# Transposing an 8192 x 8192 matrix: the loads move from ScalarE's DMA queue to SyncE's

## The chip, the core and the metric

The kernel runs on one core of one Trainium2 chip. The metric is device time in microseconds (us) of one execution, as the median of several runs. The core has a matrix engine (TensorE, PE in the profile), a vector engine (VectorE, DVE), a scalar engine (ScalarE, ACT), GpSimd (POOL) and a synchronising engine (SyncE, SP). Each works through its own list of instructions in order, and semaphores hold them together. Data moves between the main memory and the core's SBUF through 16 DMA engines. A transfer is issued by an instruction of SyncE or ScalarE and goes into that engine's queue: q1 in the profile is SyncE's, q10 is ScalarE's.

## The reference

```python
x = np.random.randn(8192, 8192).astype(np.float32)

def reference(x):
    return np.transpose(x)
```

The matrix has 268.44 MB. Each byte is read once and written once, so 536.87 MB pass through the DMA engines.

## The kernel before, in words

**Tiling.** `x` is cut into chunks of 128 rows by 4096 columns (2 MB). There are 64 chunks down (index `c`) and 2 sweeps across (index `s`), so T = 128 chunks, taken in order, a sweep at a time. A chunk is loaded with one DMA into one of three input buffers `in0` to `in2` (`load`, L100 to L104): each of the 128 partitions gets one row piece of 16 KB.

**TensorE.** `transposes` (L111 to L123) waits until the chunk's buffer is loaded (`s_ld`, L112), then makes 32 transposes of 128 x 128 through the identity matrix. They go in 8 groups of 4. Groups 0 to 3 fill the PSUM tile `ps0`, groups 4 to 7 `ps1`. Before each half it waits until the tile has been emptied (`s_bank`, L116). After each second group it counts up `s_pe`, so `s_pe` grows by 4 a chunk.

**Copies and bands.** A group is a band: 512 columns of `x`, so 512 rows of `out`. A band is gathered over 8 consecutive chunks in one of nine SBUF registers (`regs`, 2 MB each), so that a row piece of `out` in it is 4 KB long and the four rows of a partition make a run of 16 KB in SBUF. ScalarE copies bands 0 to 3 from `ps0`, VectorE bands 4 to 7 from `ps1` (L228). The bands are staggered: at each chunk one of the eight closes. In the first chunks of all and in the last ones they close with fewer chunks, hence the smaller stores of the profile, and at the change of sweep a register can hold parts of two sweeps, which are stored by two DMAs. A band that begins again takes the register that has been free longest, and its first copy waits until the store out of that register has landed (`s_st`, L202). Eight bands are open and there are nine registers, so this is the store issued two chunks before.

**Stores.** `store` (L160) is called in the order of the code right after the copies that close a band. ScalarE waits for the copy, its own or VectorE's (`s_cp`, L162), and issues the DMA into q10. The helper `wide_dma` (L28) writes the instruction directly, so that the source is one run of 16 KB in each partition; the first store of all uses the plain call (L174).

**The order around the change.** The program is unrolled in Python over the 128 chunks. For each chunk, ScalarE's list holds: its copies, the stores that close, then the wait for TensorE to have finished the chunk (L242), and the load of chunk t + 3 into the buffer that has just been read (L102). The first three loads are issued by SyncE at the start; all other loads, and all stores, are issued by ScalarE into one queue. At the end SyncE waits for the last stores (L245).

```python
            if t + NIN < T:
                nc.scalar.wait_ge(s_pe, (t + 1) * NR // 2)
                load(t + NIN)
```

The functions in full:

Of the kernel before, what the change touches and what calls it, by code (L numbers as in the profile page):

```python
# [40 lines left out]
def kernel(  # L41
# [13 lines left out]
    nc = tc.nc  # L55
# [8 lines left out]
    NR = S // B  # L64
    NIN = 3
# [4 lines left out]
    with tc.tile_critical():  # L70
# [12 lines left out]
        s_pe = nc.alloc_semaphore("s_pe")  # L83
# [15 lines left out]

        def load(t):  # L100
            s, c = chunks[t]
            (nc.sync if t < NIN else nc.scalar).dma_start(  # L102
                out=ins[t % NIN], in_=x[c * P:(c + 1) * P, s * J:(s + 1) * J]
            ).then_inc(s_ld[t % NIN], 16)  # L104

# [46 lines left out]
        for t in range(NIN):  # L152
            load(t)
# [6 lines left out]
        def store(q, e, count):  # L160
            t0, r, parts = window.pop(q)
            nc.scalar.wait_ge(s_cp[e], count)  # L162
            base = 0
            for s, a, z in parts:
                rows = (z - a) * P
                j0 = s * J + q * B * P
                dst = out[j0:j0 + B * P, a * P:a * P + rows]
                dst = dst.rearrange("(q b) i -> q b i", q=P)
                src = regs[:, r * SIZE + base:r * SIZE + base + B * rows]
                base += B * rows  # L170
                if any(stored):
                    st = wide_dma(nc, nc.scalar, "qActDynamicHW", dst, src)
                else:
                    st = nc.scalar.dma_start(  # L174
                        out=dst, in_=src.rearrange("q (b i) -> q b i", b=B)
                    )
                st.then_inc(s_st[r], 16)
                stored[r] += 1
            free.append(r)

        def closes(w, t):
            t0, r, parts = w
            return t + 1 == t0 + sum(z - a for _, a, z in parts)

        for t, (s, c) in enumerate(chunks):
            for e in range(2):
                eng = (nc.scalar, nc.vector)[e]

                place = []
                for q in range(e * NH, (e + 1) * NH):  # L190
                    if q not in window:

                        span = (q - c) % W + 1
                        r = free.pop(0)
                        parts = [(s, c, min(c + span, CH))]
                        if c + span > CH and t + span < T:
                            parts.append((s + 1, 0, c + span - CH))
                        window[q] = (t, r, parts)  # L200
                        if stored[r]:
                            eng.wait_ge(s_st[r], 16 * stored[r])  # L202
                    t0, r, parts = window[q]
                    k = [p[0] for p in parts].index(s)
                    base = r * SIZE + B * P * sum(z - a for _, a, z in parts[:k])
                    _, a, z = parts[k]
                    place.append((base + (c - a) * P, (z - a) * P))

                runs = []
                for g in range(NH):  # L210
                    if runs:
                        u = runs[-1]
                        gap = place[g][0] - place[g - 1][0]
                        if place[g][1] == place[u[0]][1] and abs(gap) < 2 ** 15 and (
                            len(u) == 1 or gap == place[u[1]][0] - place[u[0]][0]
                        ):
                            u.append(g)
                            continue
                    runs.append([g])
                for u in runs:  # L220
                    off, dist = place[u[0]]
                    gap = place[u[-1]][0] - place[u[-2]][0] if len(u) > 1 else 0
                    dims = [list(regs.ap[0]), [gap, len(u)], [dist, B], [1, P]]
                    o = bass.AP(regs.tensor, regs.offset + off, dims)
                    i = pss[e][:, u[0] * B * P:(u[-1] + 1) * B * P]
                    i = i.rearrange("p (l b i) -> p l b i", b=B, i=P)
                    eng.wait_ge(s_pe, t * NH + (e * NH + u[-1]) // 2 + 1)  # L227
                    cp = nc.scalar.copy(out=o, in_=i) if e == 0 else nc.vector.tensor_copy(out=o, in_=i)  # L228
                    ends = [e * NH + g for g in u if closes(window[e * NH + g], t)]
                    if ends:  # L230
                        cp.then_inc(s_cp[e], 1)
                        copied[e] += 1
                    if u is runs[-1]:
                        if ends:
                            eng.wait_ge(s_cp[e], copied[e])
                            eng.sem_inc(s_bank[e], 1)
                        else:
                            cp.then_inc(s_bank[e], 1)
                    for q in ends:
                        store(q, e, copied[e])  # L240
            if t + NIN < T:
                nc.scalar.wait_ge(s_pe, (t + 1) * NR // 2)  # L242
                load(t + NIN)
        for r in range(NREG):
            nc.sync.wait_ge(s_st[r], 16 * stored[r])  # L245
# [30 lines left out]
```

## Time and profile before

| what | value |
|---|---|
| median of 3 runs | 1263.75 us (1263.48 to 1265.18) |
| profiled execution, first to last instruction (span) | 1261.2 us |
| moved by DMA | 536.97 MB, mean 426 GB/s |
| read from, written to main memory | 268.44 MB, 268.44 MB |
| busy: PE, DVE, ACT | 59%, 24%, 20% |
| loads by ScalarE | 125 of 2 MB, 21.7 us from issue to landing (median) |
| loads by SyncE | 3 of 2 MB, 11.6 us |
| full stores | 114 of 2 MB, 17.5 us |
| smaller stores | 28, of 256 KB to 1792 KB |

The span is shorter than the time of a run, which also holds what lies before the first and after the last instruction; the page gives no other time of the profiled execution. The page has the span in 40 equal slices: a digit is the busy share of an engine in tenths, the row DMA the mean busy share of the 16 DMA engines, the row GB/s what they moved. The queue table lists packets, MB and the share of 16 engines' time that the packets took. A packet is one row of a transfer, here 16 KB in the steady part; a record of 4 bytes ends each engine's part of a DMA and counts up its semaphore. In the table of waits a row names the engine and line that waited, what it waited for, the total in us, how often, and the longest.

### The profile page before, as it was taken

The numbers are of one execution on the slowest core, as the hardware profiler recorded it, in microseconds if no ns is written. First come the engines' busy times: TensorE is split into PE (matmuls) and PEld (weight loads), VectorE is DVE, ScalarE is ACT, GpSimd is POOL, SyncE is SP. The second block draws the span as 40 slices with busy tenths as digits, with TensorE's granted clock in tenths as the row PEclk, the third lists the DMA queues.
The fourth block names the chain that finished last, engine by engine and source line by source line (L and its number), as shares of the span: only waits on it lengthen the run. The fifth ranks groups of instructions, "written<-read, shape, count | busy, mean of one in ns | idle before, by whom it ended". The sixth has DMA issues, their size and how long they took to land. (4 is left out here: it accounts for less than half of the span.)

```text
span 1261.2 us, 9840 instructions
## 1 busy us (share of the span) xinstructions
PE 740.3 (59%) x4096; PEld 719.8 (57%) x4096; DVE 302.7 (24%) x250; ACT 252.6 (20%) x257; POOL 0.7 (0%) x6
## 2 busy tenths in 40 slices
PE   6555655665556565665555655656566655656561
PEld 6555555665556555655555655656566655656561
DVE  3322222222222222222222222222222222222220
ACT  3212121121111211122211121121111211122120
POOL 0000000000000000000000000000000000000000
PEclk9987867777776868687776777676867677777866
DMA  9999999999999999999999999999999999999998
GB/s 386 429 427 426 430 427 429 431 428 430 431 428 431 429 429 430 430 429 430 425 423 419 431 430 429 430 430 429 431 430 429 431 429 430 430 430 429 429 429 351
DMA packets 39273, 536.97 MB, mean 426 GB/s; under 512 B 4320, under 2 KB 4832, under 8 KB 6240
## 3 DMA queue, kind: packets, MB, share of 16 engines
q10 hardware_dynamic: 38832, 530.60, 98.9%
q1 hardware_dynamic: 432, 6.29, 1.2%
q14 instruction: 8, 0.07, 0.0%
q8 instruction: 1, 0.02, 0.0%
HBM read 268.44 MB, written 268.44 MB: 426 GB/s over the span
## 5 line engine op out<-in xcount | busy, mean ns | idle before, releaser
L118 PE MATMUL ps<-ident,in 128*128 128x128 f32 x4096 | 740.3, 363 | 492.9 <-PEq L116 492.9
L118 PEld LDWEIGHTS ps<-ident,in 128*128 128x128 f32 x4096 | 719.8, 220 | 513.2 <-issue 513.2
L228 DVE COPY regs<-ps 128x512 f32<-128x512 f32 (+3 forms) x250 | 302.7, 1246 | 932.4 <-PE ps L118 780.2
L228 ACT COPY regs<-ps 128x512 f32<-128x512 f32 (+3 forms) x256 | 251.3, 1015 | 980.9 <-PE ps L118 495.5
L228 ACT ACT_TABLE_LOAD x1 | 1.3, 1283 | 0.9 <-SPq L70 0.9
L88 POOL TENSOR_SCALAR_AFFINE_SELECT ident<-ident 128x128 f32<-128x128 f32 x1 | 0.3, 292 | 0.2 <-POOL ident L86 0.2
L86 POOL MEMSET ident<- 128x128 f32 x1 | 0.2, 204 | 0.5 <-SPq L70 0.5
L260 POOL MEMSET const-bfloat16-1.0<- 128x1 bf16 x1 | 0.1, 101 | 0.0
L260 POOL MEMSET const-uint8-127<- 128x1 uint8 x1 | 0.1, 101 | 0.0
L260 POOL MEMSET const-float32-0.0<- 128x1 f32 x1 | 0.1, 98 | 0.2 <-issue 0.2
L260 POOL MEMSET const-float32-1.0<- 128x1 f32 x1 | 0.1, 98 | 0.0
## 6 DMA issues: line engine op xcount, KB each, us to landing
in<-in_x_dram ACTq DMA_DIRECT2D x125, 2048.0 KB, 21.7
out_dram<-regs ACTq DMA_DIRECT2D x114, 2048.0 KB, 17.5
out_dram<-regs ACTq DMA_DIRECT2D x4, 1792.0 KB, 17.1
in<-in_x_dram SPq DMA_DIRECT2D x3, 2048.0 KB, 11.6
out_dram<-regs ACTq DMA_DIRECT2D x4, 1536.0 KB, 15.2
out_dram<-regs ACTq DMA_DIRECT2D x4, 1280.0 KB, 15.5
out_dram<-regs ACTq DMA_DIRECT2D x4, 1024.0 KB, 15.6
out_dram<-regs ACTq DMA_DIRECT2D x4, 768.0 KB, 16.5
```

What stands on the lines that cost most here:

```text
L86: nc.gpsimd.memset(ident, 0.0).then_inc(s_id, 1)
L88: nc.gpsimd.affine_select(out=ident, in_=ident, compare_op=mybir.AluOpType.not_equal, fill=1.0, base=0, pattern=[[-1, P]], channel_multipl ...
L118: tr = nc.tensor.transpose(pss[e][:, (g * B + b) * P:(g * B + b + 1) * P], ins[k][:, q * B * P + b:(q + 1) * B * P - B + b + 1:B], ident,)
L228: cp = nc.scalar.copy(out=o, in_=i) if e == 0 else nc.vector.tensor_copy(out=o, in_=i)
L260: nc = _bacc.Bacc("TRN2", target_bir_lowering=False, num_devices=1)
```

## The change

All loads are issued by SyncE, into its own queue. The wait for TensorE, which tells that the input buffer has been read, moves to SyncE with them. Stores stay with ScalarE.

```diff
         def load(t):
             s, c = chunks[t]
-            (nc.sync if t < NIN else nc.scalar).dma_start(
+            nc.sync.dma_start(
                 out=ins[t % NIN], in_=x[c * P:(c + 1) * P, s * J:(s + 1) * J]
             ).then_inc(s_ld[t % NIN], 16)
...
             if t + NIN < T:
-                nc.scalar.wait_ge(s_pe, (t + 1) * NR // 2)
+                nc.sync.wait_ge(s_pe, (t + 1) * NR // 2)
                 load(t + NIN)
```

ScalarE's list loses 125 load instructions and the waits before them. SyncE's list grows from 3 loads to 128, with 125 waits between them. The lists of TensorE, VectorE and GpSimd are the same as before. Each of the 16 DMA engines then has packets of two queues, q1 (loads) and q10 (stores), where it had those of q10 alone once the first three loads were through.

## The prediction

> **What bounds the kernel now.** I read the page's slices and queue table first, because the busy shares of the engines (PE 59%, DVE 24%, ACT 20%) leave no engine as the bound.
>
> ```profile
> DMA  9999999999999999999999999999999999999998
> GB/s 386 429 427 426 430 427 429 431 428 430 431 428 431 429 429 430 430 429 430 425 423 419 431 430 429 430 430 429 431 430 429 431 429 430 430 430 429 429 429 351
> ...
> q10 hardware_dynamic: 38832, 530.60, 98.9%
> q1 hardware_dynamic: 432, 6.29, 1.2%
> ```
>
> The sixteen DMA engines are busy in every slice, at 429 to 431 GB/s outside a few slices, and nearly all of it is one queue, q10, that of ScalarE. q1 is SyncE's: the first three loads.
>
> Next the waits. They say whether a chunk (2 MB in, 2 MB out) waits for anything that is not a transfer.
>
> ```profile
> DVE regs L228 <- PE ps L118: 780.2, 120, 13.2
> PEld ps L118 <- issue: 513.2, 127, 8.4
> ACT regs L228 <- PE ps L118: 495.5, 100, 9.2
> PE ps L118 <- PEq L116: 492.9, 127, 8.5
> ACT regs L228 <- DMA out_dram<-regs: 473.9, 60, 10.4
> DVE regs L228 <- DMA out_dram<-regs: 152.1, 23, 7.8
> ```
>
> TensorE waits 127 times, once a chunk, for the next load; the copies wait for TensorE or for an old store. All of it ends in a transfer. The timeline shows one chunk:
>
> ```profile
> 600.53 6.49 PE L118 MATMUL ps<-ident,in 128*128 128x128 f32 x32 [3.50 <-PEq L116]
> ...
> 606.00 2.48 DVE L228 COPY regs<-ps 128x512 f32<-128x512 f32 x4 [7.32 <-PE ps L118]
> 608.52 0.55 ACTq L28 DMA_DIRECT2D out_dram<-regs  x1
> 609.11 0.62 ACTq L102 DMA_DIRECT2D in<-in_x_dram  x1
> 610.27 5.21 PE L118 MATMUL ps<-ident,in 128*128 128x128 f32 x32 [3.26 <-PEq L116]
> ```
>
> The period is 610.27 - 600.53 = 9.74 us, and 4.194 MB in 9.74 us is 430.6 GB/s: the chunk is the transfer. 128 chunks of 9.74 are 1246.7 of the span of 1261.2.
>
> Last the packets. In the trace's packet records one engine's share of a chunk is 8 load and 8 store packets of 16 KB, back to back. A load packet takes 611 ns; a store packet takes 611 ns for the first two of a DMA and 616 for the other six. So **the time of one 16 KB packet is the kernel's time**: 1 ns on each of the 16 costs 128 x 16 = 2.05 us.
>
> **The change, part by part.** Arithmetic, sizes, packets and buffers stay; the instruction order of TensorE, VectorE and GpSimd stays too.
>
> *Issues.* 125 loads leave ScalarE's order (637 ns median, 4589 longest, L102) and go to SyncE, where the first three took 372 to 426 ns each. One issue in 9.74 us hides there. Behind SyncE's new wait (the count s_pe, L242) stand only later loads and the last waits for stores, which nothing else needs. ScalarE gets back under 1 us in most chunks, but its copies already wait 473.9 us for stores and 495.5 for TensorE: worth 0. If that cover were gone, it would be 0.6 us a chunk.
>
> *Load earlier.* L102 stands behind a store that needs VectorE's copy, so at 609.11 it comes 2.1 us after TensorE is through (600.53 + 6.49 = 607.02). SyncE issues it at about 607. It then lies behind other packets anyway (21.7 us from issue to landing, of which its own 2 MB take 4.9): worth 0. Only the start has a hole that this might fill: 21 to 24 us runs at 328 GB/s, which is (430 - 328)/430 x 3 = 0.7 us. The packets there are slow (839 ns in 22 to 23 us), not missing, so I take 0 and keep 0.7 for the range.
>
> *Stores.* Nine registers serve eight open bands, so the copy of chunk t needs the store of chunk t - 2. A store may take about two periods less the copies, 19.5 - 3 = 16.5 us, and takes 17.5 now. With two queues its 8 packets alternate with loads, 16 x 0.61 = 9.8 us plus what stores are ahead: it lands sooner. An engine idles only if both its queues are empty. Loads have three buffers, of which TensorE holds one for 6 us in 9.74, so their queue stays full. Worth 0.
>
> *Alternation.* This term decides, and the steady trace has no example. The nearest rows are two.
>
> First, at 15 to 17.8 us the last of SyncE's loads meet the first store, ScalarE's 512-byte packets, on the same engines.
>
> ```profile
> 3.00:14.00 11.00, 5.54 (x33) 5.57 (x34) 0.78 (x2) 2.15 (x4) 0.00 (x0) 1.00 1.00 429
> 14.00:18.00 4.00, 4.00 (x34) 3.83 (x32) 2.61 (x5) 2.15 (x4) 0.00 (x0) 1.00 0.96 378
> ```
>
> (Columns: window, its length, busy us of five engines, clock, DMA share, GB/s.) The packet records show one packet of one queue, then one of the other. 72 load packets end in this stretch, mean 633.3 ns; the 296 before it had 611.7. So **21.6 ns a load packet**. The store packets cost what all 512-byte packets cost, 27 ns. Most of the extra sits at one place: 13 packets that start at 15.3 to 15.65 us carry 1461 of the 1604 ns by which the 72 are over 611, the other 59 next to nothing.
>
> Second, eight instruction fetches of 8 KB (q14) fall among q10's packets after the start. Each took 309 ns, and the q10 packet that came next took 796 to 1039 ns: 185 to 428 above 611, mean 301. This is the dear end: a return to a queue after a large packet of another.
>
> The ends: nothing (the others of the 72), and 301 ns at each return, which would be 301 x 2 x 8 x 128 = 617 us. The first row excludes the latter, since there alternating returns cost almost nothing. I take its mean, for it is the nearest: two hardware queues, a load and a store. 125 loads x 8 packets x 21.6 ns = **+21.6 us**. I give stores nothing extra; the same price for them would add another 21.
>
> The Trainium skill, "DMA: Bandwidth & Descriptors", section "Queues, rings and completion order", puts the switch elsewhere: the engine leaves a queue only at packet boundaries, and a packet is typically 9 to 17 descriptors. By that a DMA's share of eight rows would go through whole, there would be an eighth of the switches, and this term would be 21.6 / 8 = 2.7 us, an estimate from that page. The records speak against it: in the stretch with both queues each 16 KB row was followed by a row of the other queue, so the sum keeps 21.6.
>
> *What alternation gives back.* The slower store packets come only after two stores in a row; with a load between them they should all take 611. 10,121 packets had 616: x 5 ns / 16 engines = **-3.2 us**.
>
> *Sum.* +21.6 - 3.2 = +18.4 on the span of 1261.2: 1279.6. The median of the runs, 1263.75, lies 2.55 above the span; the profile's page has no other time of this execution, so I take these 2.55 as what lies around it. **1282 us**, 1.5% slower.
>
> **Rivals.**
>
> *Alternation is free: faster.* The price of 21.6 was one event at the first store, not one at every switch. Without it the extra is (1604 - 1461)/(72 - 13) = 2.4 ns a load packet, 2.4 us in all, against -3.2 and up to -0.7 for the start: 1262.2; with none at all 1263.75 - 3.9 = 1259.9. For it: the plain 611s in the alternating stretch. Against it: those store packets were 512 bytes and left the load stream almost whole. It decides when the extra of a load packet is under 1.4 ns, since 1000 of them in a row on an engine make 1.0 us a ns and 3.9 - 1.4 is the 2.5 us that can be told. Chance 0.15.
>
> *No change.* All issues end on the same engines, packets have the same bytes, and 611 and 616 stay as they are: within 2.5 us of 1263.75. The Trainium skill, "DMA: Bandwidth & Descriptors", section "Issuing engines are not separate DMA queues", has this as its rule: transfers from several issuers interleave on the same engines and only issue time is saved. The trace agrees on the same engines and on the interleaving, not on the rate, which is 378 against 429 in the one window with both queues. Chance 0.2.
>
> *Reads and writes in mixture cost more: clearly slower.* Today the engines mostly load together, then store together. Where they drift apart there are clusters of packets of 700 to 1700 ns:
>
> ```profile
> 200.00:600.00 400.00, 239.34 (x1312) 232.73 (x1312) 97.05 (x77) 79.23 (x73) 0.00 (x0) 0.75 1.01 430
> 640.00:690.00 50.00, 28.68 (x159) 27.84 (x158) 12.23 (x17) 9.39 (x6) 0.00 (x0) 0.71 1.01 419
> ```
>
> At 419 throughout: 1246.7 x (430/419 - 1) = +32.7, so 1296. If one queue ran dry once a chunk and its return cost 301 ns, it would be 128 x 0.301 = +38.5, so 1302. Both: 1335. Against: between 700 and 1200 us one engine is 5.3 us behind the rest (the spread of a DMA's sixteen completions), loads beside their stores, and the rate is 430 still. Chance 0.2.
>
> *The change doesn't take hold*, because SyncE issues late or both share a queue: q1 exists and carried its loads at 429 GB/s. Chance under 0.01, within "no change".
>
> **Chances and range.** The forecast (some price per switch, 1267 to 1290) 0.45, with the rivals at 0.2 clearly slower, 0.2 the same, 0.15 faster. A difference under 0.2% (2.5 us) is about what a measurement of this kernel cannot tell from no change. So slower 0.65, same 0.2, faster 0.15. The range reaches down to 1259, the free case with all gains, and up to 1322, between one of the dear costs and both.
>
> **What would show it.** Queue table: q1 and q10 at about half the packets each. Landing: stores fall from 17.5 us, loads stay near 21. If the forecast is right, DMA stays at 9 in every slice while GB/s falls to about 423, and 16 KB packets average some 10 ns more in the steady part. If a queue runs dry, the DMA share drops. If alternation is free, store packets are 611 and the chunk period is 9.71 us. The forecast is wrong if 16 KB stores beside loads cost either nothing or much more than 512-byte ones, which no row of this trace shows.

## The result and the profile after

The changed kernel took 1274.8 us in the median of 13 runs (1265.31 to 1276.88), the kernel before 1264.4 (1262.6 to 1269.07). The ratio is 1.0055, 95% interval 1.0037 to 1.0073. The 13 runs lie in two groups with nothing between them: six at 1265.3 to 1266.7 (mean 1266.2), seven at 1274.8 to 1276.9 (mean 1275.8). So there are two things to explain: 9.7 us that come or stay away, and some 2 us that are always there.

The profile after is of the upper group, with a span of 1273.0. Its page:

```profile
DMA  9799999999999999999999999999999999999998
GB/s 395 304 429 428 430 432 428 429 430 428 430 431 429 429 429 429 430 431 428 428 421 417 430 423 430 429 429 429 428 429 423 428 429 424 429 425 428 428 400 365
...
q1 hardware_dynamic: 18432, 268.44, 49.7%
q10 hardware_dynamic: 20832, 268.44, 49.7%
```

The packets are now half and half, as the change says, and most slices still run at 428 to 432 GB/s. One slice stands out, the second (32 to 64 us): 304 GB/s, and the DMA engines, which were at 9 everywhere, are at 7. The windows around it, before (first fence) and after (second), have in their last two columns the DMA share and GB/s:

```profile
15.00:34.00 19.00, 16.17 (x117) 15.69 (x117) 8.48 (x15) 7.89 (x13) 0.00 (x0) 0.91 1.01 410
34.00:62.00 28.00, 15.14 (x108) 14.50 (x107) 9.46 (x13) 6.49 (x7) 0.00 (x0) 0.94 1.01 429
```

```profile
15.00:34.00 19.00, 7.11 (x57) 6.76 (x56) 5.66 (x10) 2.15 (x4) 0.00 (x0) 0.78 1.00 414
34.00:62.00 28.00, 18.42 (x128) 18.10 (x128) 8.93 (x14) 10.32 (x13) 0.00 (x0) 0.84 0.75 297
```

In 28 us at 297 instead of 429 GB/s, (429 - 297)/429 x 28 = 8.6 us are lost. That is most of the 11.8 us between the two spans. In the 19 us ahead of it, the transfers are as fast as in the kernel before (414 and 410), but TensorE (first column of busy time) does 7.11 us of work where it did 16.17. The timeline after says what it waited for (a row can stand for several instructions: the SyncE row is seven loads, the first of them, load 3, issued at 14.17):

```profile
11.16 0.64 ACTq L174 DMA_DIRECT2D out_dram<-regs  x1
...
14.17 44.55 SPq L102 DMA_DIRECT2D in<-in_x_dram  x7
...
34.12 1.56 ACT L228 COPY regs<-ps 128x512 f32<-128x512 f32 x3 [16.18 <-DMA out_dram<-regs]
...
37.03 14.31 PE L118 MATMUL ps<-ident,in 128*128 128x128 f32 x96 [14.51 <-PEq L116]
```

The first store, 256 KB, is issued at 11.16 and lands at 34.1 (by its semaphore). It landed at 18.8 before. ScalarE's copy of chunk 2 needs the register behind that store and waits 16.18 us; TensorE needs the PSUM tile behind that copy and waits 14.51. With TensorE idle no further load is issued: load 5 goes out at 22.55, load 6 only at 43.62. The packet records are empty from 34.8 to 36.9 us, and again from 38.9 to 43.6. In the kernel before, the same copy waits only 1.75 us, and for TensorE:

```profile
11.06 0.65 ACTq L174 DMA_DIRECT2D out_dram<-regs  x1
...
14.18 0.35 ACTq L102 DMA_DIRECT2D in<-in_x_dram  x1
...
19.70 1.56 ACT L228 COPY regs<-ps 128x512 f32<-128x512 f32 x3 [1.75 <-PE ps L118]
```

Load 3 is issued at the same time there (14.18), but into the store's own queue, behind it. Once load 2's last packet has gone through q1, at 17.75, nothing stands beside the store.

Why the small store was slow is in the packet records. It is the one plain store of the kernel (L174), so it goes as 512 packets of 512 bytes, 32 for each of the 16 DMA engines. The engines take a packet of q10 and a packet of q1 in turn, and one of q1 is 16 KB: between 18 and 33 us the records hold 365 load packets and 368 of the store's. So 32 packets of 27 ns need up to 32 turns of 611 + 27 ns, an estimate of 20 us. In the records they run from 15.1 to 33.6 us. **The turns are fair by packet, not by byte**: in its turns q1 moved 32 times as much as the store.

The chain that ended last shows what this does to the order of work, before (first) and after:

```profile
by line: DMA out_dram<-regs 1.4%; PE ps L118 0.4%; DVE regs L228 0.3%; issue 0.0%; DVEq L227 0.0%
```

```profile
by line: DMA out_dram<-regs 84.9%; DVE regs L228 4.5%; ACT regs L228 3.8%; PE ps L118 1.0%; ACTq L28 0.4%; issue 0.3%; ACTq L236 0.0%; DVEq L227 0.0%
```

Before, the end is traced back only through the last store and copies to TensorE's work at 1208 us, where the trail of releasers ends. After, the chain store, copy, store runs back to 37 us, where TensorE takes up work again after the stall.

### The profile page after: what moved, and what is told of

It is laid out like the page before. It is cut to its first block, busy times and chain, and to the rows that moved or that the text cites. A ratio compares the mean times of both kernels' runs of the same rounds, so it can differ in the third digit from the quotient of the medians.

```text
span 1273.0 us, 9840 instructions
## 1 busy us (share of the span) xinstructions
PE 716.7 (56%) x4096; PEld 693.5 (54%) x4096; DVE 302.0 (24%) x250; ACT 252.2 (20%) x257; POOL 0.7 (0%) x6
## 4 chain that ended last, share of the span: by engine, by line
DMA 85%; DVE 5%; ACT 4%; PE 1%; ACTq 0%; issue 0%; DVEq 0%
DMA out_dram<-regs 85%; DVE regs L228 5%; ACT regs L228 4%; PE ps L118 1%; ACTq L28 0%; ACTq L236 0%; DVEq L227 0%
## 5 line engine op out<-in xcount | busy, mean ns | idle before, releaser
L118 PE MATMUL ps<-ident,in 128*128 128x128 f32 x4096 | 716.7, 354 | 527.6 <-PEq L116 527.2
L118 PEld LDWEIGHTS ps<-ident,in 128*128 128x128 f32 x4096 | 693.5, 218 | 550.7 <-issue 550.7
## 6 DMA issues: line engine op xcount, KB each, us to landing
in<-in_x_dram SPq DMA_DIRECT2D x128, 2048.0 KB, 17.8
out_dram<-regs ACTq DMA_DIRECT2D x114, 2048.0 KB, 17.7
out_dram<-regs ACTq DMA_DIRECT2D x4, 1536.0 KB, 17.5
```

Of the source, the lines that this page charges most:

```text
L118: tr = nc.tensor.transpose(pss[e][:, (g * B + b) * P:(g * B + b + 1) * P], ins[k][:, q * B * P + b:(q + 1) * B * P - B + b + 1:B], ident,)
```

## The experiments

The theory after the first look: large packets alternate at no price, and the time goes in the start, through the first store's small packets. Its rival is the forecast's own term, a price on every switch in the steady part.

**The same kernel again.** No edit.

> The changed kernel once more, unchanged, for a second profile: its runs lie in two groups, near 1266 and near 1275 us, and the profile at hand is of the slower group. If this run falls near 1266: the theory of the start (the first store's 512-byte packets take turns with 16 KB load packets and hold up the copies) expects the hole in the DMA between 34 and 62 us to be smaller or missing there; a rival, that the two groups differ in the last 60 us (where the DMA engines idle some 4 us around 1234 and 1242 us), expects the same hole at the start and no idle at the end. If it falls near 1275, both expect the profile at hand again.

1267.14 us, the lower group, and the start is whole: 425 GB/s from 34 to 62 us. The end is as it was, a DMA share of 0.93 from 1200 to 1250 us (0.94 in the profile after), so the rival that puts the difference there is out. But the theory's first form ("the hole is there") is not enough, since the code is the same. The timeline of this run:

```profile
11.16 0.64 ACTq L174 DMA_DIRECT2D out_dram<-regs  x1
...
15.14 45.38 SPq L102 DMA_DIRECT2D in<-in_x_dram  x8
...
20.36 1.56 ACT L228 COPY regs<-ps 128x512 f32<-128x512 f32 x3 [1.45 <-PE ps L118]
```

The store is issued at the same time, load 3 0.97 us later, because TensorE was later through chunk 0. Its transposes start 213 ns apart at first and 120 ns apart from some moment on: after 17 of them in the profile after, after 28 in this one, so that the 32nd starts at 13.85 and at 14.83. Why the pace changes when it does, no run here shows (the granted clock is 1.00 in both profiles from 8 to 15.5 us).

Now q1 runs dry: load 2's last packet ends at 17.8 us and load 3's first starts at 18.16. In the 0.4 us between, the small packets go one after another, the store lands at 18.85, and the copy of chunk 2 runs at 20.36 with no wait for it. **Two groups, one race**: issued at 14.17, load 3 follows load 2 without a gap; issued at 15.14, it comes too late for that, and the store gets through.

**The first store in larger packets.** Sixteen of 128 partitions stay plain, the rest goes in runs of 2 KB: 4 + 7 packets an engine, not 32.

```diff
-                    st = nc.scalar.dma_start(out=dst, in_=src...)
+                    nc.scalar.dma_start(out=dst[:16], in_=src[:16]...).then_inc(s_st[r], 16)
+                    stored[r] += 1
+                    st = wide_dma(nc, nc.scalar, "qActDynamicHW", dst[16:], src[16:])
```

> The first store goes out as 4 plain packets and 7 packets of 2 KB on each DMA engine, where it had 32 of 512 bytes; all else as in the changed kernel. Theory of the start: the first store lands near 22 us where it landed at 34, the copy that waits 16 us for it waits under 5, the DMA hole at 34 to 62 us goes, and the time falls by about 9 us against the changed kernel's runs near 1275, to 1264 to 1267. Rival, that alternation in the steady part costs the time: less than 1 us is won.

1268.43 us (1267.57 to 1268.72, five runs), none in the upper group; ratio 1.0035, 1.0021 to 1.0049. The store landed at 22.2 and the copy waited 3.94 us, as expected, but the time is 1.4 us over the range. Load 3 is issued at 14.34 in this profile, and q1 is empty from 17.67 to 17.76 us, so whether this profile would have stalled with the narrow store is not shown.

**Which part of the chunks.** The loads from 16 on in SyncE's queue, and the complement. The waits move with the loads, here and in the runs below.

```diff
-            nc.sync.dma_start(
+            (nc.sync if t < NIN or t >= 16 else nc.scalar).dma_start(    # late_sync
+            (nc.sync if t < 16 else nc.scalar).dma_start(                # early_sync
```

> Loads 3 to 15 stay on ScalarE's queue as before, loads from 16 on go to SyncE's: alternation in 112 of 128 chunks, but not at the start. Theory of the start: 1262 to 1267 us, the start as before the change. Rival, alternation in the steady part: the loss of about 10 us stays to seven eighths, 1272 to 1275.

> The complement: loads 0 to 15 on SyncE's queue, all later ones on ScalarE's as before. Theory of the start: the hole at 34 to 62 us is there and the time is 1272 to 1275 us, although only 13 of 128 chunks are changed. Rival, alternation in the steady part: 1264 to 1266.

late_sync: 1268.85 us, ratio 1.0045, 1.0032 to 1.0059. early_sync: 1271.97 us, at the edge of its range (all five at 1271.4 to 1273.7), ratio 1.0067, 1.0054 to 1.0081. In the profile of early_sync the hole is there (299 GB/s from 34 to 62 us). So 13 chunks of 128 lose more than the other 112, as the theory of the start wants, but late_sync is 2 us over its range: something outside the start costs as well. That all five runs of early_sync have the time of a stall, where seven of 13 runs of the changed kernel do, is not explained.

**Load 3 held back.** SyncE waits for a quarter of chunk 1 as well.

```diff
-                nc.sync.wait_ge(s_pe, (t + 1) * NR // 2)
+                nc.sync.wait_ge(s_pe, (t + 1) * NR // 2 + (t == 0))
```

> The changed kernel, but SyncE issues load 3 only when TensorE is a quarter into chunk 1 (s_pe at 5, not 4), about 1.2 us later; loads 4 on as they were. In the profiles so far the start stalls when load 3 is issued at 14.0 or 14.17 us and does not when it is issued at 15.14: issued early, its packets reach q1 before load 2's last ones (17.4 us) are gone, q1 never runs dry, and the first store's 512-byte packets get one turn in two until 33.6 us. By this theory all runs lie in the lower group, 1265 to 1269 us, none at 1275, and the first store lands near 19 us. Rival, that the two groups come from something else (the clock, the memory): both groups again, about half and half.

**q1 kept full.** The other way: 512 KB that nobody reads go into q1 ahead of load 2. The tile `pad` is made larger for it, and SyncE waits for it at the end.

```diff
             if t == NIN - 1:
+                nc.sync.dma_start(out=pad, in_=x[0:P, 0:1024]).then_inc(s_pad, 16)
```

> The changed kernel with one more load, of 512 KB that nobody reads, in q1 between loads 1 and 2: 1.3 us more for q1, so that load 2's packets last until about 19 us and load 3, whether it is issued at 14.0 or at 15.2, always finds q1 full. Theory of the start: the first store then always takes turns with load packets, lands after 34 us, and every run is in the upper group, 1274 to 1279 us, none near 1266. With the run that held load 3 back, where none was near 1275, this sets the groups both ways. Rival, that the groups come from something else: both groups, moved up by the 1.3 us of the added load, 1267 and 1277.

Held back: nine runs, all at 1265.6 to 1267.5 us, ratio 1.0023, 1.0013 to 1.0033. Kept full: four runs, all at 1275.9 to 1277.7, ratio 1.0100, 1.0083 to 1.0116. The window of the start in the run held back (first fence) and in the one kept full:

```profile
34.00:62.00 28.00, 17.40 (x111) 16.73 (x110) 8.87 (x12) 7.71 (x8) 0.00 (x0) 0.82 1.01 425
```

```profile
34.00:62.00 28.00, 18.30 (x128) 17.97 (x128) 7.96 (x13) 10.32 (x13) 0.00 (x0) 0.82 0.74 292
```

A shift of one or two microseconds in one queue puts all runs into the one group or all into the other. The two profiles issue load 3 at 14.66 (held back) and at 14.63 (kept full), so it is not the time of issue itself that decides, but whether q1 still has packets: load 2's last packet ends at 17.82 in the one and at 19.76 in the other. Over all profiles in which load 3 goes to q1, q1 runs dry in the six where load 3 was issued 1.8 to 3.3 us before that end, and not in the three with 3.6 us or more. This settles what makes the groups.

**The suspected cost doubled, with a control.** The second store plain too: 32 packets of 1 KB an engine, not 8 of 4 KB, in the changed kernel and in the one before.

```diff
-                if any(stored):
+                if sum(stored) > 1:
```

> The changed kernel with the second store plain as well: its 512 KB go as 32 packets of 1 KB on each DMA engine, where they went as 8 of 4 KB. Theory, that a store of many small packets beside a full load queue is slow because turns are by packet: each packet waits for a 16 KB load packet, 32 x 0.63 = 20 us for the second store in every run, the copies of chunk 3 wait for it, and the time rises to between 1272 and 1290 us. Rival, that small packets only cost their own transfer time: 24 more packets per engine, under 1 us.

> The control: the kernel before, with one queue, and the same plain second store. One queue serves the 32 small packets one after another, so the theory of turns expects no stall: within 1.5 us of the kernel before. Rival, that small packets are slow to write by themselves: as much slower as in the other kernel.

With two queues 1275.77 us (1272.63 to 1276.88), ratio 1.0098, 1.0083 to 1.0114. The copies of chunk 3 wait for the second store, as foretold:

```profile
40.40 1.99 ACT L228 COPY regs<-ps 128x512 f32<-128x512 f32 x3 [17.70 <-DMA out_dram<-regs]
```

In this profile the first store landed in time (18.8 us, load 3 issued at 14.71), so this stall is the second store's alone. It is that of the fastest of the four runs, 1272.63 us; whether the first store stalled as well in the others is not shown. With one queue the same edit gives 1263.72 us, ratio 0.9998, 0.9988 to 1.0007: nothing. So the small packets are not slow by themselves here; they are when they take turns with large ones.

**Alternation alone.** Loads 0 to 55 in SyncE's queue with load 3 held back, the rest as before the change.

```diff
+            (nc.sync if t < 56 else nc.scalar).dma_start(                # and the wait likewise
```

> Loads 0 to 55 on SyncE, with load 3 held back as in the run before, loads from 56 on ScalarE's queue as before the change: the steady part of the first sweep alternates, 16 KB loads against 16 KB stores, and start stall, change of sweep, second sweep and end are out of it. Theory, that large packets alternate at no cost: 1263 to 1265 us, the same as the kernel before within 0.1%, and the 16 KB packets between 100 and 530 us at 611 to 616 ns. Rival, the prediction's 21.6 ns for each load packet: 53 x 8 x 21.6 ns = 9.2 us slower.

1266.32 us, ratio 1.0016, 1.0002 to 1.0029: a little slower than the kernel before, 1.3 us over the theory's range, and far from the rival's 9.2. The stretch that this run is about is clean. The same window before, after and here:

```profile
100.00:530.00 430.00, 259.07 (x1408) 251.97 (x1408) 102.41 (x73) 84.81 (x71) 0.00 (x0) 0.75 1.01 429
```

```profile
100.00:530.00 430.00, 252.08 (x1408) 244.98 (x1408) 101.31 (x72) 85.52 (x73) 0.00 (x0) 0.77 1.01 429
```

```profile
100.00:530.00 430.00, 259.43 (x1402) 252.53 (x1403) 102.25 (x73) 84.77 (x71) 0.00 (x0) 0.73 1.01 430
```

By the packet records of that stretch a load packet took 611.4 ns after and a store packet 615.0, mean 613.2; before, all packets together had 613.6. **The switch between two queues costs nothing here**, and the 0.4 ns that it gives back would be 0.8 us over the run. In this run load packets took 611.3 and store packets 615.1. By 1200 us it had moved 513.25 MB, the kernel before 513.18, so what this profile loses (its span is 1263.6, against 1261.2) it loses after 1200 us, where all its transfers are in one queue again.

**The rest of the loss: second sweep and end.** Three runs looked for the 2.5 us that are left when the start is whole: only the last 16 loads in SyncE's queue, all but the last 16, and only loads 72 to 111.

```diff
+            (nc.sync if t < NIN or t >= 112 else nc.scalar).dma_start(        # tail_sync
+            (nc.sync if t < 112 else nc.scalar).dma_start(                    # no_tail_sync, load 3 held back
+            (nc.sync if t < NIN or 72 <= t < 112 else nc.scalar).dma_start(   # second_sweep_sync
```

> The kernel before, with only loads 112 to 127 moved to SyncE. The profiles with loads on SyncE show DMA engines idle for 3 to 4 us between 1225 and 1245 us. Theory, that this comes from the two queues at the end: the same idle time here, partly made good by engines that end together, 1264 to 1267 us. Rival, that it is left over from what the second sweep did before: no idle time, 1263 to 1264.

> Loads 0 to 111 on SyncE with load 3 held back, the last 16 on ScalarE's queue as before. Theory, that what is left of the loss after the start (2.5 us) is half slow load packets in the second sweep and half idle engines at the end: 1264.5 to 1266 us, between the kernel before and the run with load 3 held back, and no idle DMA slice between 1220 and 1245 us. Rival, that the idle time at the end costs nothing in sum, since all engines then end together: 1266 to 1267.5, as with load 3 held back.

> Only loads 72 to 111 on SyncE: the steady part of the second sweep, with one change of queue at its beginning. If what is slow in the second sweep is the queues there, slow load packets (over 640 ns) appear between 750 and 1100 us and the time is 1264.5 to 1267 us. If it was left behind by the change of sweep with two queues, this part is as clean as the first sweep's, and the time is 1263.5 to 1265 us, less what the hand-over at load 72 costs (0 to 2 us).

| run | us | ratio | 95% interval |
|---|---|---|---|
| tail_sync | 1264.42 | 1.0008 | 0.9999 to 1.0017 |
| no_tail_sync | 1268.77 | 1.0033 | 1.0019 to 1.0047 |
| second_sweep_sync | 1264.95 | 0.9998 | 0.9985 to 1.0011 |

Neither part alone costs what is missing. In second_sweep_sync one load packet of 4134 between 750 and 1100 us took over 640 ns, against 110 of 4578 in the profile after and 3 of 4584 with load 3 held back (in q10 45 of 5017, against 7 in each of those two): with the same two queues the slow packets come and go. The window 1200 to 1250 us, before (first), with load 3 held back (second) and with the last 16 loads given back (third):

```profile
1200.00:1250.00 50.00, 22.96 (x123) 22.28 (x122) 9.68 (x12) 8.69 (x16) 0.00 (x0) 0.67 1.00 424
```

```profile
1200.00:1250.00 50.00, 22.90 (x135) 21.48 (x133) 11.85 (x14) 10.65 (x20) 0.00 (x0) 0.73 0.90 381
```

```profile
1200.00:1250.00 50.00, 24.66 (x133) 23.83 (x131) 11.66 (x14) 10.46 (x20) 0.00 (x0) 0.69 0.99 422
```

The idle time near the end is real with two queues all the way (0.90) and goes when the last 16 loads are given back (0.99). But tail_sync has two queues there too, and 0.98: its time is in the theory's range, yet the idle time that the theory wanted is nearly missing, so two queues at the end do not make it by themselves. And no_tail_sync is slower, not faster: both hypotheses about it fail. It lost its time elsewhere: 399 GB/s from 15 to 34 us (416 with load 3 held back), 421 from 700 to 800 (428) and 427 from 800 to 1080 (430).

The bytes moved by 1200 us say where the rest is lost, but not always the same place: 513.18 MB before and 513.15 with load 3 held back, so the 2.9 us between these two spans (1261.2 and 1264.1) are lost after 1200 us; 511.95 in the second run of the changed kernel, which is 2.9 of its 4.1 us, lost earlier. The profiles also show that the sixteen engines drift apart: the completions of one DMA near 1200 us are spread over 5.3 us before, up to 10.0 with load 3 held back, 7.3 in first_sweep_sync. That every part of the end waits for the slowest engine is an argument, not a test. What causes the last 2 to 3 us stays open.

## Why the prediction was wrong, step by step

The forecast was 1282 us, slower by 18.4 us on the span. Slower is right, but by luck: the measured difference is 10.4 us in the medians (7.0 by the ratio), the term that made the forecast slower measured nothing, and what was lost comes from a place that the forecast had at 0.

- **What bounds the kernel**: right. The steady part stayed at 429 GB/s and nothing on the compute engines mattered there.
- **Issues** and **load earlier** at 0: right. At the start load 3 is not even issued earlier (14.17 after, 14.18 before). What does the harm is its queue: it no longer stands behind the first store but beside it, and when it comes soon enough it closes the gap in q1 that the store needs.
- **Alternation, +21.6 us: the step that failed.** It took a cluster of 13 slow packets for a price per switch. In the steady part after the change, where loads and stores take turns (16 of each in 1.2 us), a load packet took 611.4 ns: 0.4 ns over 611, not 21.6. Beside the first store's 512-byte packets, from 15.1 to 33.6 us, 414 of 439 load packets took 611.2 ns in the mean; the other 25 are over 640, 23 of them at 31.5 to 32.9 us. A cluster like it is in all 14 profiles, 1 to 3 us before q1 has sent its last packet for the time being: at about 15.5 us in the 11 in which nothing follows load 2 at once, at 30 to 34 us in the three in which load 3 does. So it comes where the queue runs out, not at every switch; its cause is open. The text had the right reading as a rival ("one event at the first store") and gave it 0.15, but that rival's faster time did not come either.
- **What alternation gives back, -3.2 us**: wrong as well. With loads between them store packets took 615.0 ns in the mean, where the forecast had 611.
- **Stores, worth 0 ("it lands sooner", "An engine idles only if both its queues are empty")**: the missing term, worth 9.7 us in the runs that stall. Both queues did run empty. The estimate of the landing was made for 8 packets of 16 KB and used for every store. For those the turns did no harm (the median landing is 17.7 us after, 17.5 before, so no sooner either); the first store has 32 packets of 512 bytes an engine and needs 32 turns. The row was at hand: the forecast used just these packets to price a switch, noted that one took turns with one, and did not ask when the last of the 32 would be through: at 33.6 us.
- **The rule of the Trainium skill** weighed there, "DMA: Bandwidth & Descriptors", section "Queues, rings and completion order" (a queue keeps the engine for a packet of typically 9 to 17 descriptors): no trace here agrees on that size. As many rows of 16 KB as of 512 bytes went through between 18 and 33 us (365 and 368), so a turn was one row. Its other half, round robin by packet, is what decides the start.
- **No change**, with the rule of the Trainium skill, "DMA: Bandwidth & Descriptors", section "Issuing engines are not separate DMA queues", that several issuers only save issue time: the trace agrees for the steady part (429 GB/s with one queue and with two) and not for the start, where the store landed at 34.1 us and not at 18.8.
- **Reads and writes in mixture cost more**: refuted in the first sweep, 100 to 530 us, where loads and stores alternate: 429 GB/s, and 3 of 11270 packets over 640 ns, 44 of 11266 before. In the second sweep slow load packets come and go between profiles with the same queues (110 and 3, above), so mixture alone is not their cause; what is stays open.
- **What would show it**: half the packets each, right; GB/s at about 423 all through, wrong: 428 to 432 in most slices, and one slice at 304. Stores did not fall from 17.5 us (17.7), and loads did not stay near 21 (17.8).

## What to carry to other kernels

In these runs two queues on the same DMA engines shared them by packet. Equal packets of 16 KB took turns at no cost (613.2 ns a packet, 613.6 in one queue). A small transfer in small packets beside a full queue of large ones waited one large packet for each of its own: 32 of them took 18.5 us. So count the packets per engine of a small transfer, multiply by the other queue's packet time, and ask who waits for its end. One queue, in which an urgent transfer stands ahead of a later bulk load, keeps an order that two queues give up; no run with loads in SyncE's queue was faster than the kernel before beyond its interval. And where the runs of a kernel fall into two groups, compare a profile of each: here one load's issue time, 0.97 us apart, led to a stall of some 9 us.

## What was not expected of the hardware

Reads and writes in turn ran as fast as one queue did before: 429 GB/s. In the kernel before, an instruction fetch of 8 KB (q14) among q10's packets made the next packet 185 to 428 ns longer, while the alternation of q1 and q10 made none longer: 2 of 5635 load packets and 1 of 5635 store packets between 100 and 530 us took over 640 ns in the profile after, and each of the three began as one of three such fetches ended. When q1 was running dry, load 3's first packet came 2.1 to 3.4 us after its issue (16.07 to 18.12 in no_tail_sync, 14.71 to 18.13 in the run with two plain stores).
